# One gated MLP layer on one core: the second block's x transposed by DMA in 16-bit planes instead of by TensorE

## The chip, the cores and the metric

The kernel runs on one NeuronCore of a Trainium2 chip. The metric is the device time of one execution in microseconds (us); less is better. The engines are TensorE (PE in the profile; its weight loads are PEld), VectorE (DVE), ScalarE (ACT), GpSimd (POOL) and SyncE (SP), which issues all DMAs of this kernel from one queue, in order.

## The reference, cut to what matters

With D = 1024, E = 2048, 2048 positions and one layer, all in float32:

```python
mod = silu(c) @ ada_w + ada_b
shift, scale, gate = split(mod, 3)
h = rmsnorm(x, norm_g) * (1 + scale) + shift
u, v, z = split(h @ w_in, 3)              # 1024 -> 3 * 2048
u = gelu(u)
v = layernorm(gelu(v), ln_g, ln_b)        # over the 2048 columns
v = einsum("hpq,bnqhc->bnphc", sp_w, v)   # 128-position chunks, 8 head groups
v = v + sp_b
y = (u * v * silu(z)) @ w_out             # 2048 -> 1024
x = x + gate * y
return rmsnorm(x, final_g)
```

## The kernel before, in words

The 2048 positions are worked on in two blocks of TB = 1024 (b = 0 and 1). Each block first makes v (`project_v`), then a u and a z unit for each of 8 head groups (`project` for the products, `after` for the gating), sixteen units in all (NU = 16). The products use a Strassen scheme with seven products p1 to p7 of quarter matrices. Each float32 operand is split in a rounded part `hi` on ACT and a remainder `lo` on DVE (`split`, L168 and L169), and three matmuls of 128x512 stand for one (`mm3`, L178 to L180). Twelve such matmuls make one product of a unit. Four buffers each hold `hi` and `lo`. The output projection follows after both blocks.

`project_v` runs a list of steps. For block 0 the list `seq_0` is: p1 and p2 of v group 1 (`v1`), then p5, p6, p3, p7, p4 of group 0 (`v0`), then the same five of group 1. After step n it calls `hook_0(n)`, which issues loads, Strassen sums and, from n = 4 to 10, steps of the generator `preparations()`. The product p1 of group 1 of block 0 comes too early to be kept on the chip: it is stored in `c1_dram` ("spilled") and loaded again when p6 of this group is evicted (L496 to L500). In `evict`, p6 adds its PSUM bank to c1 and the sum to u4.

`finish` puts a piece of v through Gelu, takes its `bn_stats` (L516) and stores it in `v_dram`. `layer_norm` (L708) aggregates the statistics of the eight chunks of 128 positions with `bn_aggr` (L710) and makes mean and rstd, and `load_v` loads a head group of v again and normalizes it on ACT (L538).

`preparations()` prepares, beside block 0, what block 1 needs. After three steps for the spatial weights it runs `prepare_h(tp)` for the eight chunks tp of 128 positions of block 1. This loads x (128 x 1024) into the one buffer of the tag `hx`, normalizes it (`normalize_x`: Square with a running sum on ACT, L157; a power on POOL, L150; the product on DVE, L160), transposes it on PE in eight 128x128 pieces, four to a PSUM bank (L667), applies scale and shift on ACT out of PSUM (`modulate`, L253), and stores the result in `h_dram`. Later `prepare_sums` loads quarters of `h_dram`, forms Strassen sums and stores these, and at the last unit of block 0 `refill` loads them as the left operands of block 1. `preparations()` is advanced by `hook_0`, and then twice in each unit: in `after`, behind its second step, and at its end in `side`.

Short-lived tiles (products, gating results, the Square's output, transposed pieces, parts of sums) come from one ring of 15 buffers of 2 KB per partition (`c_tile`).

The order on each engine is laid down ahead of the run by the scheduler of the framework. It goes by the order in which the program names the operations and by its own idea of when each can start, so operations named later may stand ahead of ones that wait. At run time each engine and the DMA queue of SP keep to the order laid down.

Of the kernel before, what the change touches and what calls it, by code (L numbers as in the profile page):

```python
# [9 lines left out]
F32 = mybir.dt.float32  # L10
F32R = mybir.dt.float32r
BF16 = mybir.dt.bfloat16
AF = mybir.ActivationFunctionType
ALU = mybir.AluOpType
PSUM = bass.MemoryType.PSUM
# [2 lines left out]
P = 128  # L18
# [4 lines left out]
def kernel(  # L23
# [33 lines left out]
    nc = tc.nc  # L57

    T, D = x.shape
# [6 lines left out]
    KD = D // P  # L66
# [20 lines left out]
    def acc_bank(name):  # L87
        return acc.tile([P, 512], F32, tag="acc", name=name)

    def aux_bank(name):  # L90
        return aux.tile([P, 512], F32, tag="aux", name=name)
# [71 lines left out]
    def normalize_x(xt, name):  # L163
        for _ in normalize_steps(xt, name):
            pass
# [16 lines left out]
    def c_tile(name, shape=(P, HT), dt=F32):  # L182
        return cp.tile(list(shape), dt, tag="c", name=name)
# [68 lines left out]
    def modulate(out, src, k):  # L252
        nc.scalar.activation(  # L253
            out, src, AF.Identity, bias=mshift[:, k:k + 1], scale=mscale[:, k:k + 1]
        )
# [170 lines left out]
    class Group:  # L426
# [5 lines left out]
        def __init__(self, b, g):  # L432
            self.b, self.g = b, g
            self.name = f"{b}_v_{g}"
            self.q, self.c1, self.u4 = {}, {}, {}
            self.spilled = b == 0 and g == 1

        def load(self, r, f, slot):
# [26 lines left out]
        def multiply(self, p, k, w):  # L465
            if k == 0:
                self.po = [acc_bank(f"{p}_{ch}_{self.name}") for ch in range(HT // P)]
            hi, lo = S[Group.LEFT[p]][k]
            for ch, ps in enumerate(self.po):
                cs = slice(ch * P, (ch + 1) * P)  # L470
                mm3(ps, hi[:, cs], lo[:, cs], *w, k == 0, k == KH - 1)
            if k == KH - 1:
                for ch, ps in enumerate(self.po):
                    self.evict(p, ch, ps)

        def evict(self, p, ch, ps):
            def tile(name):
                return c_tile(f"{name}_{ch}_{self.name}", (P, FB))

            def add(t, s, o=None):  # L480
                nc.vector.tensor_tensor(t if o is None else o, t, s, op=ALU.add)  # L481

            if p == "p1":
                self.c1[ch] = tile("c1")
                nc.scalar.activation(self.c1[ch], ps, AF.Copy)
                if self.spilled:
                    nc.sync.dma_start(c1_dram[ch], self.c1[ch])
            elif p == "p2":
                t = tile("c11")
                add(self.c1[ch], ps, t)  # L490
                self.finish(0, 0, ch, t)
            elif p == "p5":
                self.u4[ch] = tile("u4")
                nc.scalar.activation(self.u4[ch], ps, AF.Copy)
            elif p == "p6":
                if self.spilled:  # L496
                    self.c1[ch] = tile("u2")
                    nc.sync.dma_start(self.c1[ch], c1_dram[ch])
                add(self.c1[ch], ps)
                add(self.u4[ch], self.c1[ch])  # L500
            elif p == "p3":
                t = tile("c12")
                add(self.u4[ch], ps, t)
                self.finish(0, 1, ch, t)
            elif p == "p7":
                add(self.u4[ch], ps)
                self.finish(1, 1, ch, self.u4[ch])
                add(self.c1[ch], ps)
            else:
                add(self.c1[ch], ps)  # L510
                self.finish(1, 0, ch, self.c1[ch])

        def finish(self, m, f, ch, t):
            i, n = 2 * self.g + f, m * (HT // P) + ch
            nc.scalar.activation(t, t, AF.Gelu_apprx_tanh)
            nc.vector.bn_stats(stats[:, n, i, :], t)  # L516
            nc.sync.dma_start(v_dram[i][:, n, :], t)

    def project_v(seq, hook, right=()):

# [133 lines left out]

    def prepare_h(tp):

        xt = vp.tile([P, D], F32, tag="hx", name=f"x_1_{tp}", bufs=1)
        t0 = TB + tp * P
        nc.sync.dma_start(xt, x[t0:t0 + P, :])
        normalize_x(xt, f"1_{tp}")  # L660
        yield
        for i in range(KD // 4):
            ps = aux_bank(f"psh_{tp}_{i}")
            ht = c_tile(f"ht_{tp}_{i}", (P, 4, P))
            for kk in range(4):
                k = 4 * i + kk
                nc.tensor.transpose(ps[:, kk * P:(kk + 1) * P], xt[:, k * P:(k + 1) * P], ident)  # L667
            for kk in range(4):
                modulate(ht[:, kk, :], ps[:, kk * P:(kk + 1) * P], 4 * i + kk)
            nc.sync.dma_start(h_dram[:, 4 * i:4 * i + 4, tp * P:(tp + 1) * P], ht)  # L670
            yield

    def prepare_sums(k):

        t = []
        for r, kk in ((0, k), (0, k + KH), (1, k), (1, k + KH)):
            t.append(c_tile(f"hq_{kk}_{r}"))
            nc.sync.dma_start(t[-1], h_dram[:, kk, r * HT:(r + 1) * HT])
        t.append(c_tile(f"hq_{k}_s"))
        strassen_sums(  # L680
            *t[:4], t[4], t[2], t[0], t[1],
            lambda i, s: nc.sync.dma_start(hs_dram[i][k], s),
        )
# [22 lines left out]


    def layer_norm():  # L708
        for ch in range(NCH):
            nc.vector.bn_aggr(mv[:, ch, :], stats[:, ch])  # L710
        nc.vector.tensor_scalar(lm, mv[:, :, 1], EPS, None, op0=ALU.add)
        nc.gpsimd.tensor_tensor(lr, lm, mhalf, op=ALU.pow)
        nc.vector.tensor_scalar(lm, mv[:, :, 0], -1.0, None, op0=ALU.mult)
        nc.gpsimd.tensor_tensor(lm, lm, lr, op=ALU.mult)
# [166 lines left out]
    def hook_0(n):  # L881

        if n == 0:
            v0.load(1, 1, "raw0")
        elif n == 1:
            v0.load(1, 0, "raw1")
        elif n == 3:
            v1.load(0, 0, "raw1")
        elif n == 4:
            v1.load(0, 1, "raw0")  # L890
        elif n == 5:
            v1.load(1, 1, "v1")
        elif n == 6:
            v1.load(1, 0, "v0")
        elif n == 10:
            units[0].load()
            units[0].p1()
        if n != 1:
            sums_0(n)
        for j in ahead_loads.get(n, ()):  # L900
            units[2 * j].ahead_load()
        if 4 <= n < 11:
            next(prep, None)
        if 8 <= n < 11:
            next(prep, None)

    def side(i):

        next(prep, None)
        if i in (4,6,9,11):  # L910
            prepare_sums((4,6,9,11).index(i))
        if 0 <= i - NU < KD:
            for db in range(NDB):
                prepare_gate(NDB * (i - NU) + db, gate_sum)
        elif i - NU == KD:
            finish_gate(gate_sum)
# [449 lines left out]
```

## Time and profile before

| what | value |
|---|---|
| median of 3 runs | 1339.7 us (1339.46 to 1340.07) |
| the profiled execution | 1338.98 us, its span 1337.2 us |
| PE busy | 1309.1 us, 98% of the span |
| DVE busy | 1078.7 us, 81% |
| ACT busy | 684.7 us, 51% |
| POOL busy | 25.6 us, 2% |
| DMA | 229.24 MB, mean 171 GB/s |

A time of the span starts at the first instruction of the profiled execution. A matmul's duration in the trace overlaps with the next one's, so what matmuls cost is read from the distance between their starts. The transposes of block 1's x run between 189 and 337 us of the span.

### The profile page before, as it was taken

How to read it: one execution, taken by the hardware profiler on the slowest of the kernel's cores; microseconds unless marked ns; L12 is line 12 of the kernel's file. 1: busy time of each engine (PE TensorE's matmuls, PEld its weight loads, DVE VectorE, ACT ScalarE, POOL GpSimd, SP SyncE). 2: the span in 40 equal slices, each digit the busy share in tenths (PEclk: the TensorE clock that was granted, in tenths of full speed). 3: DMA queues.
4: the chain of work that ended last, by engine and by line, in shares of the span. 5: the costliest groups of instructions: out<-in, count | busy, mean ns of one | idle time of the engine just before them, and what ended most of it. 6: DMA issues, size and time to landing. Idle time of an engine off the chain costs nothing.

```text
span 1337.2 us, 17243 instructions
## 1 busy us (share of the span) xinstructions
PE 1309.1 (98%) x6078; PEld 1088.8 (81%) x6078; DVE 1078.7 (81%) x1801; ACT 684.7 (51%) x1177; POOL 25.6 (2%) x42
## 2 busy tenths in 40 slices
PE   5999999999999999999999999999999999999998
PEld 4878877888888888888888888888888888888886
DVE  6889978888889888978688889887799944757875
ACT  5775446766545536534345555445543434344553
POOL 0000001000000000000000000000000000000101
PEclk9999999999999999999999999999999999999999
DMA  9771657456665446442243445434338722235733
GB/s 322 262 268 62 221 181 229 155 175 222 230 210 201 157 163 235 183 142 95 96 158 102 147 154 185 138 122 127 123 118 310 265 95 95 96 119 210 255 108 126
DMA packets 156799, 229.24 MB, mean 171 GB/s; under 512 B 9188, under 2 KB 91172, under 8 KB 153384
## 3 DMA queue, kind: packets, MB, share of 16 engines
q1 hardware_dynamic: 156712, 228.14, 49.9%
q8 instruction: 47, 0.77, 0.2%
q14 instruction: 40, 0.33, 0.1%
HBM read 160.47 MB, written 67.64 MB: 171 GB/s over the span
## 4 chain that ended last, share of the span: by engine, by line
PE 77%; DVE 3%; DMA 2%; issue 1%; ACT 1%; POOL 0%; POOLq 0%; SPq 0%; DVEq 0%; ACTq 0%
PE p_z L180 7%; PE p_z L178 7%; PE p_z L179 7%; PE po L180 7%; PE po L179 7%; PE po L178 7%; PE p_u L180 6%; PE p_u L178 6%; PE p_u L179 6%; PE pmix_u L553 4%; PE p_v L178 4%; PE p_v L179 3%; PE p_v L180 3%; DMA vn<-v_dram 1%; DMA held<-g_dram 1%
## 5 line engine op out<-in xcount | busy, mean ns | idle before, releaser
L178 PE MATMUL p_v<-hi_p_v,sh 128*128 128x512 f32 x416 | 162.5, 391 | 2.9 <-DVE u_v L481 2.3
L180 PE MATMUL po<-hi_o,gl 128*128 128x512 f32 x416 | 161.9, 389 | 0.4 <-DVE gl L169 0.4
L179 PE MATMUL p_v<-lo_p_v,sh 128*128 128x512 f32 x416 | 162.3, 390 | 0.0
L180 PE MATMUL p_v<-hi_p_v,sl 128*128 128x512 f32 x416 | 162.3, 391 | 0.0
L179 PE MATMUL po<-lo_o,gh 128*128 128x512 f32 x416 | 161.8, 389 | 0.0
L178 PE MATMUL po<-hi_o,gh 128*128 128x512 f32 x416 | 161.8, 389 | 0.0
L168 ACT ACTIVATE gh<-gr 128x1024 fp32r<-128x1024 f32 x52 | 55.0, 1059 | 126.2 <-PE po L179 116.4
L168 ACT ACTIVATE hi_p_v<-b_v 128x512 fp32r<-128x512 f32 x104 | 65.0, 630 | 106.2 <-PE p_v L180 89.7
L169 DVE TENSOR_TENSOR gl<-gr,gh 128x1024 fp32r<-128x1024 f32 x52 | 63.5, 1222 | 60.0 <-ACT gh L168 59.8
L169 DVE TENSOR_TENSOR lo_p_v<-b_v,hi_p_v 128x512 fp32r<-128x512 f32 x104 | 69.9, 687 | 34.4 <-ACT hi_p_v L168 34.1
L178 PEld LDWEIGHTS p_v<-hi_p_v,sh 128*128 128x128 f32 x416 | 78.1, 188 | 20.3 <-DVE u_v L481 2.8
L180 PEld LDWEIGHTS po<-hi_o,gl 128*128 128x128 f32 x416 | 78.1, 188 | 16.9 <-DVE gl L169 0.8
L179 PEld LDWEIGHTS po<-lo_o,gh 128*128 128x128 f32 x416 | 78.1, 188 | 16.4
L178 PEld LDWEIGHTS po<-hi_o,gh 128*128 128x128 f32 x416 | 78.1, 188 | 16.2
L179 PEld LDWEIGHTS p_v<-lo_p_v,sh 128*128 128x128 f32 x416 | 78.1, 188 | 16.1 <-DVE lo_p_v L169 0.2
L180 PEld LDWEIGHTS p_v<-hi_p_v,sl 128*128 128x128 f32 x416 | 78.1, 188 | 16.0
L538 ACT ACTIVATE vn<-vn,lm,lr 128x256 f32<-128x256 f32 x128 | 67.7, 590 | 27.1 <-DMA vn<-v_dram 18.6
L180 PE MATMUL p_u<-sh,lo_p_u 128*128 128x512 f32 x196 | 76.5, 390 | 0.0
L179 PE MATMUL p_u<-sl,hi_p_u 128*128 128x512 f32 x196 | 76.3, 389 | 0.0
L178 PE MATMUL p_u<-sh,hi_p_u 128*128 128x512 f32 x196 | 76.3, 389 | 0.0
L178 PE MATMUL p_z<-sh,hi_p_z 128*128 128x512 f32 x192 | 74.9, 390 | 0.0
L180 PE MATMUL p_z<-sh,lo_p_z 128*128 128x512 f32 x192 | 74.7, 389 | 0.0
(244 smaller groups left out, 3096.5 us busy)
## 6 DMA issues: line engine op xcount, KB each, us to landing
gr<-g_dram SPq DMA_DIRECT2D x26, 1024.0 KB, 4.8
b_v<-in_gm_w_in_dram SPq DMA_DIRECT2D x18, 1024.0 KB, 6.1
vn<-v_dram SPq DMA_DIRECT2D x16, 1024.0 KB, 6.0
raw_u<-in_gm_w_in_dram SPq DMA_DIRECT2D x16, 1024.0 KB, 5.1
raw_z<-in_gm_w_in_dram SPq DMA_DIRECT2D x16, 1024.0 KB, 5.2
v_dram<-c_v SPq DMA_DIRECT2D x44, 256.0 KB, 2.7
g_dram<-c_u SPq DMA_DIRECT2D x37, 256.0 KB, 2.3
aw<-in_ada_w_dram SPq DMA_DIRECT2D x16, 512.0 KB, 5.1
```

The source lines that it names most:

```text
L168: nc.scalar.activation(hi, src, AF.Copy)
L169: nc.vector.tensor_tensor(lo, src, hi.bitcast(F32), op=ALU.subtract)
L178: nc.tensor.matmul(ps, lhsT=sh, rhs=mh, start=first, stop=False)
L179: nc.tensor.matmul(ps, lhsT=sh, rhs=ml, start=False, stop=False)
L180: nc.tensor.matmul(ps, lhsT=sl, rhs=mh, start=False, stop=last)
L538: nc.scalar.activation(vt[:, ch, :], vt[:, ch, :], AF.Identity, bias=lm[:, ch:ch + 1], scale=lr[:, ch:ch + 1],)
L553: nc.tensor.matmul(pm[:, i * P:(i + 1) * P], lhsT=vt[:, m * (NCH // 2) + i, f * P:(f + 1) * P], rhs=spT[:, u.j, :], start=True, stop=True,)
```

## The change

The changed kernel does four things otherwise.

- `prepare_h` no longer uses PE. After the normalization ACT copies the low and the high 16-bit halves of x's float32 words into two planes of 128 x 1024 16-bit numbers. Each plane is transposed by a DMA from SBUF to SBUF, issued by SP. In the next step POOL copies the two transposed planes, interleaved, back into the buffer of x, so that this now holds the transposed float32 numbers. ACT applies scale and shift in place, eight times 128x128, and one DMA stores all of it.
- The load of x is a step of its own in the generator, ahead of the normalization, so `prepare_h` has three steps, of which `preparations()` still takes two in one place. `hook_0` advances the generator seven times instead of ten, and `prepare_sums` runs at units 6, 8, 10 and 12 instead of 4, 6, 9 and 11.
- The spilled p1 is loaded again in p6's second slice k = 1, not at p6's eviction.
- The `bn_aggr` of a chunk is issued with the chunk's last `bn_stats` instead of in `layer_norm`.

```diff
-            self.q, self.c1, self.u4 = {}, {}, {}
+            self.q, self.c1, self.u4, self.left = {}, {}, {}, {}
...
         def multiply(self, p, k, w):
             if k == 0:
                 self.po = [acc_bank(f"{p}_{ch}_{self.name}") for ch in range(HT // P)]
+            if self.spilled and p == "p6" and k == 1:
+                for ch in range(HT // P):
+                    self.c1[ch] = c_tile(f"u2_{ch}_{self.name}", (P, FB))
+                    nc.sync.dma_start(self.c1[ch], c1_dram[ch])
...
             elif p == "p6":
-                if self.spilled:
-                    self.c1[ch] = tile("u2")
-                    nc.sync.dma_start(self.c1[ch], c1_dram[ch])
                 add(self.c1[ch], ps)
...
             nc.sync.dma_start(v_dram[i][:, n, :], t)
+            self.left[n] = self.left.get(n, 2) - 1
+            if self.g and not self.left[n]:
+                nc.vector.bn_aggr(mv[:, n, :], stats[:, n])
...
         nc.sync.dma_start(xt, x[t0:t0 + P, :])
+        yield
         normalize_x(xt, f"1_{tp}")
+        turned = []
+        for i in range(2):
+            plane = c_tile(f"plane_{tp}_{i}", (P, D), U16)
+            nc.scalar.activation(plane, xt.bitcast(U16)[:, i::2], AF.Copy)
+            turned.append(c_tile(f"turned_{tp}_{i}", (P, KD, P), U16))
+            nc.sync.dma_start_transpose(turned[i], plane)
         yield
-        for i in range(KD // 4):
-            ps = aux_bank(f"psh_{tp}_{i}")
-            ht = c_tile(f"ht_{tp}_{i}", (P, 4, P))
-            for kk in range(4):
-                k = 4 * i + kk
-                nc.tensor.transpose(ps[:, kk * P:(kk + 1) * P], xt[:, k * P:(k + 1) * P], ident)
-            for kk in range(4):
-                modulate(ht[:, kk, :], ps[:, kk * P:(kk + 1) * P], 4 * i + kk)
-            nc.sync.dma_start(h_dram[:, 4 * i:4 * i + 4, tp * P:(tp + 1) * P], ht)
-            yield
+        ht = xt.rearrange("p (k t) -> p k t", t=P)
+        for i in range(2):
+            nc.gpsimd.tensor_copy(ht.bitcast(U16)[:, :, i::2], turned[i])
+        for k in range(KD):
+            modulate(ht[:, k, :], ht[:, k, :], k)
+        nc.sync.dma_start(h_dram[:, :, tp * P:(tp + 1) * P], ht)
+        yield
...
     def layer_norm():
-        for ch in range(NCH):
-            nc.vector.bn_aggr(mv[:, ch, :], stats[:, ch])
...
         if 4 <= n < 11:
             next(prep, None)
-        if 8 <= n < 11:
-            next(prep, None)
...
-        if i in (4,6,9,11):
-            prepare_sums((4,6,9,11).index(i))
+        if i in (6, 8, 10, 12):
+            prepare_sums((6, 8, 10, 12).index(i))
```

## Rows read from the trace of the kernel before

**Rows 1.** The page: busy time and share of the span, by engine.
```profile
PE 1309.1 (98%) x6078; PEld 1088.8 (81%) x6078; DVE 1078.7 (81%) x1801; ACT 684.7 (51%) x1177; POOL 25.6 (2%) x42
```

**Rows 2.** Waits of PE: total us, times, longest.
```profile
PE p_v L178 <- DVE u_v L481: 2.3, 1, 2.3
PE psh L667 <- DVE x L160: 1.1, 2, 0.6
PE p_u L180 <- DVE lo_b_u L169: 0.9, 1, 0.9
```

**Rows 3.** Timeline of PE: start, us, line, operation, count.
```profile
210.72 0.40 PE L180 MATMUL p_v<-hi_p_v,sl 128*128 128x512 f32 x1
210.95 1.04 PE L667 MATMUL psh<-ident,x 128*128 128x128 f32 x8
211.74 0.48 PE L178 MATMUL p_v<-hi_p_v,sh 128*128 128x512 f32 x1
212.06 0.39 PE L179 MATMUL p_v<-lo_p_v,sh 128*128 128x512 f32 x1
...
249.92 1.05 PE L553 MATMUL pmix_u<-spT,vn 128*128 128x128 f32 x8
250.81 0.60 PE L667 MATMUL psh<-ident,x 128*128 128x128 f32 x4
251.17 0.48 PE L178 MATMUL p_z<-sh,hi_t_z 128*128 128x512 f32 x1
...
254.02 1.05 PE L553 MATMUL pmix_u<-spT,vn 128*128 128x128 f32 x8
254.83 0.48 PE L178 MATMUL p_z<-sh,hi_t_z 128*128 128x512 f32 x1
...
267.19 0.39 PE L178 MATMUL p_u<-sh,hi_b_u 128*128 128x512 f32 x1
```

**Rows 4.** Timelines of SP and DVE around the spilled product's reload.
```profile
186.31 2.64 SPq L498 DMA_DIRECT2D u_v<-c_dram  x4
...
192.34 0.69 DVE L481 TENSOR_TENSOR u_v<-u_v,p_v 128x512 f32<-128x512 f32 x1 [3.44 <-DMA u_v<-c_dram]
```

**Rows 5.** The chain that ended last, from 218.65 to 231.58 us (first, one, last).
```profile
218.68 0.15 DVE r_m L149
...
229.94 0.37 DVE mv L710 x2
...
231.58 0.50 PE p_u L180
```

**Rows 6.** Stretches: PE, PEld, DVE, ACT, POOL busy (instructions), clock, DMA share, GB/s.
```profile
183.00:232.00 49.00, 45.62 (x208) 36.26 (x207) 37.33 (x72) 28.83 (x59) 3.81 (x5) 1.00 0.72 239
232.00:271.00 39.00, 38.43 (x192) 32.09 (x191) 32.35 (x53) 28.09 (x55) 2.16 (x3) 1.00 0.51 168
...
310.00:349.00 39.00, 39.00 (x196) 32.95 (x195) 34.11 (x55) 25.39 (x49) 0.55 (x1) 1.00 0.61 192
```

**Rows 7.** Groups by line and shape: busy us, mean ns.
```profile
L168 ACT ACTIVATE gh<-gr 128x1024 fp32r<-128x1024 f32 x52 | 55.0, 1059 | 126.2 <-PE po L179 116.4 <-issue 7.2 <-DVE t_u L559 2.5
L253 ACT ACTIVATE ht<-psh,mshift,mscale 128x128 f32<-128x128 f32 x64 | 24.4, 457 | 2.5 <-PE psh L667 2.4
L160 DVE TENSOR_SCALAR x<-x,r 128x1024 f32<-128x1024 f32 x16 | 12.0, 751 | 6.8 <-POOL r L150 6.6
masks.py:199 POOL TENSOR_SCALAR_AFFINE_SELECT ident<-ident 128x128 f32<-128x128 f32 x1 | 0.3, 294 | 0.1
masks.py:197 POOL MEMSET ident<- 128x128 f32 x1 | 0.2, 205 | 0.3 <-POOLq L1345 0.3
```

**Rows 8.** Timeline of DVE: the remainder used by PE behind 267.19 us.
```profile
258.49 0.68 DVE L169 TENSOR_TENSOR lo_b_u<-raw_u,hi_b_u 128x512 fp32r<-128x512 f32 x1
```

**Rows 9.** DMA queue (packets, MB, share of 16 engines) and issues (count, KB, us to landing).
```profile
q1 hardware_dynamic: 156712, 228.14, 49.9%
...
hs_dram<-hq SPq DMA_DIRECT2D x12, 256.0 KB, 2.1
```

More of the change, by code (lines that the diff above doesn't have):

```diff
@@ L12 @@
 BF16 = mybir.dt.bfloat16
+U16 = mybir.dt.uint16
 AF = mybir.ActivationFunctionType
```

## The prediction

> **What bounds the kernel now.** I read the page first: PE is busy 98% of the span [rows 1], so time is gained where PE's work or its waits go away, and lost where a new wait reaches PE. Then the list of PE's waits: behind the start-up it waits three times in the stretch that the change touches, 2.3 us for the reload of the spilled product, 1.1 us (two times) for a normalized x ahead of its transposes, and 0.9 us for a remainder at the first u unit [rows 2]. The timeline of PE gives what a transpose costs between matmuls [rows 3]. The chain that ended last runs on PE except, here, from 218.68 to 231.5 us, where it is on DVE [rows 5]. The stretches tell how much room the other engines have: from 183 to 232 us DVE is busy 37.3 of 49 us, and in the pairs of a u and a z unit of 39 us it is busy 32 to 34 and ACT 25 to 28 [rows 6].
>
> **The transposes go from PE.** Without them a matmul starts 0.23 us after the one before (210.72 to 210.95). A run of 8 transposes holds back the next matmul by 211.74 - 210.95 = 0.79 us, and the matmul after that starts 0.32 us later, not 0.23: together 0.88 us [rows 3]. In front of the units there are three such runs: 2.6 us. In the units there are ten runs of 4. With one, behind a mix of 8, the next product starts 251.17 - 249.92 = 1.25 us after the mix, without one 254.83 - 254.02 = 0.81 us: 0.44 us each, 4.4 us in all [rows 3]. PE's two waits for x have nothing to wait for any more: 1.1 us [rows 2]. Sum: 8.1 us. Bounds: 7.0 us, if other waits take the place of these, and 8.4 us, if the short gaps ahead of two runs go as well.
>
> **The reload is issued earlier.** The four loads go out at 186.31 us, and the first eviction on DVE waits 3.44 us for them and starts at 192.34 us; this is PE's wait of 2.3 us, because no bank is free [rows 4, 2]. A product of this group takes four slices of twelve matmuls, 2.7 us each by the 0.23 us above; behind k = 1 three slices are still to be run, so the loads leave some 8 us earlier than the eviction asks for them. They took 6 us (186.31 to 192.34). I take the whole 2.3 us. Lower bound 0, if SP stands behind another wait at that time. The four tiles lie in the ring 8 us longer; I cost that at nothing because only the four sums of p5 are kept beside them.
>
> **The aggregates and the stretch where DVE sets the end.** Two of the aggregates stand in DVE's chain at 229.94 us with 0.37 us, and a normalization of the fourth chunk too [rows 5]. The new program runs two normalizations ahead of the units, not four: 2 x 0.75 us of DVE less [rows 7]. Against it stand POOL's copies of the first chunk, which are new work beside DVE. I take 0.5 of the 0.9 us that PE waits at the end of this chain [rows 2]; bounds 0 and 0.9.
>
> **What is added, and on whom.** ACT: two plane copies of 1024 elements a chunk, no such row exists; by a 128x1024 copy they take 1.06 us each [rows 7], 2.1 us a chunk and 17 us in all. The eight modulates stay, from SBUF now, by the row of before 0.46 us [rows 7]. In a pair of units two chunks are prepared: ACT goes from 25 to 28 us to some 30 to 32 of 39 us [rows 6]. Work that hides it: ACT and DVE run ahead of PE. The remainder made at 258.49 us belongs to the product that PE begins at 267.19 us, 8.7 us later [rows 8, 3]. If that cover were gone, a chunk would cost PE the 2.1 us, 17 us in all. POOL: two copies of 1024 16-bit elements. The nearest rows are a fill of 128 elements, 205 ns, and a select of 128 elements, 294 ns [rows 7], 1.6 to 2.3 ns an element with all fixed time in them; as an upper bound a copy takes 2.3 us, and as a lower 0.9 us, because a fixed part must be in the 205 ns. I take 1.4 us; POOL is idle there [rows 6]. SP: two transposes more a chunk, one store of 512 KB in place of two of 256 KB, and x's load, which must wait until the store has read the buffer; behind these stand weight loads and stores of the gating in the same queue. The transposes themselves have no row. Lower bound 2.1 us, the fastest landing of 256 KB [rows 9]. By the queue's row a packet takes 0.499 x 16 x 1337.2 us / 156712 = 68 ns of an engine; a plane in rows of 256 bytes is 1024 packets, 64 an engine, 4.4 us, and in single elements 131072 packets, 560 us, which no row excludes [rows 9]. I take 4.4 us, because a plane moves in pieces of 128 elements if its blocks are 128x128. Between the two steps of a chunk lie five products (of twelve matmuls, 2.7 us each), or four where a saved product is skipped: 11 to 14 us. The chain to the planes' end takes 1.06 (Square) + 0.75 + 2 x 1.06 = 3.9 us and some 1 us for the statistics and the power; two transposes bring it to 10 to 14 us. That is about as long as the distance, so the merge comes at its time or a little late, inside the cover of 8.7 us. For all this new work together I take 2 us on PE, 0.25 us a chunk; bounds 0, because the units' only PE waits in the list are those for x [rows 2], and 17 us.
>
> [...]
>
> **Sum.** 8.1 + 2.3 + 0.5 - 2.0 = 8.9 us. The profiled execution took 1338.98 us, of which 1337.2 us are the span; it would come to 1330.1 us. The median of the runs lies 0.7 us above it, so I predict 1339.7 - 8.9 = 1330.8 us.
>
> **The rivals.**
>
> *DVE gives back what PE gains* (17%). [...] I split this case 8, 5 and 4 over faster, same and slower. [...]
>
> *The transposes land later than the order allows for, and ACT stands before the modulates* (12%, slower 10, same 2). In-order queues make it a wait: behind the modulates stand the `hi` parts and evictions, behind the store on SP the weight loads. If the merge comes d us later than its place in the order, each chunk costs PE d - 8.7 us. It becomes slower than before at 8 x (d - 8.7) > 10.9, d over 10 us, which means a plane of about 10 us, not 4.4. At d = 13 us the time is 1339.7 - 10.9 + 34 = 1363 us. For it: the price of a transpose is unknown. Against it: the queue has room, its engines are busy half to three quarters of the time here [rows 6].
>
> *The gain is given back later* (8%, faster 6, same 2). The stage in front of the units gets shorter on PE, and the chain moves to DVE there: only the units' 4.4 + 1.1 us and part of the rest remain, 1334 to 1337 us.
>
> *The ring is full* (5%, same 3, slower 2). A chunk takes five of fifteen tiles, not three, and holds four of them through the transposes, while u, z and the next u hold up to twelve. A bank that finds no tile is not evicted, and PE waits; at 1 to 2 us a chunk the time is 1338 to 1346 us.
>
> **How the numbers follow.** The forecast has 58%. A measurement of this kernel tells 0.2%, 2.7 us, from no change. Faster (under 1337.0 us): 58 + 8 + 6 = 72%. Same: 5 + 2 + 2 + 3 = 12%. Slower (over 1342.4 us): 4 + 10 + 2 = 16%. The likeliest case's own range is 1327.5 us (all gains, no new wait: 8.4 + 2.3 + 0.9 = 11.6 us, and 0.6 us for an order that happens to fall better) to 1335 us. The range is 1327 to 1341 us: it leaves out the slower cases and 4% below.
>
> **What would show it.** Right: no transposes of `psh` on PE; PE's wait for the reload and its waits for x gone; the first u unit some 5 us earlier, the end of the seventh unit some 9 us earlier, and from there the same distances as before; transposes landing in under 5 us; ACT's modulates with no wait over 8 us. Wrong: PE waiting for `hi` or `lo` or an eviction between 190 and 380 us; DVE operations longer beside POOL's copies; ACT waiting for POOL, and POOL for the transposes, by 10 us and more; SP standing at a transpose or at x's load with weight loads behind it.

## The result and the profile after

The changed kernel takes 1360.2 us, the kernel before, measured beside it, 1339.6 us: ratio 1.0148, interval 1.0135 to 1.016. It is 20.6 us slower where 8.9 us less were forecast. The page of the changed kernel, engines and granted clock in 40 slices (in tenths of full speed; answers to [rows 1]):

```profile
PE 1311.4 (97%) x6014; PEld 1085.4 (80%) x6014; DVE 1084.9 (80%) x1801; ACT 700.6 (52%) x1193; POOL 48.2 (4%) x58
...
PEclk9999999998899999999999999999999999999999
```

The span went from 1337.2 to 1358.9 us, by 21.7. PE's time without work (span less busy) went from 28.1 to 47.5 us, by 19.4, and its busy time rose by 2.3 us although 64 transposes are gone [rows 1]. Its four longest groups of waits from 150 to 540 us (answers to [rows 2]):

```profile
PE p_z L179 <- DVE c_u L321: 12.8, 2, 7.5
PE p_z L181 <- DVE lo_p_z L170: 3.2, 3, 1.4
PE p_z L179 <- ACT c_z L378: 2.2, 2, 1.1
PE p_u L181 <- DVE lo_t_u L170: 1.3, 1, 1.3
```

The waits of [rows 2] for the reload and for x are gone, as forecast. In their place stand two long waits for `c_u`, the sum with a saved product (the p1 of a u unit, made ahead, kept in DRAM and loaded again by SP, L375), and a number of short ones. Stretches (answers to [rows 6]):

```profile
232.00:271.00 39.00, 38.13 (x184) 31.50 (x183) 35.17 (x55) 28.95 (x54) 4.24 (x5) 1.00 0.62 179
310.00:349.00 39.00, 30.92 (x137) 24.77 (x136) 28.47 (x43) 21.98 (x38) 6.82 (x6) 0.91 0.58 152
349.00:388.00 39.00, 31.21 (x135) 25.46 (x133) 25.56 (x40) 24.80 (x44) 4.22 (x4) 0.87 0.68 202
```

From 310 to 349 us PE is busy 30.9 us, not 39.0 [rows 6], and DVE and ACT do less work too: nobody is overloaded, everybody waits. The single operations cost about what was forecast. DMA issues (count, KB, us to landing), and POOL's group by line:

```profile
h_dram<-x SPq DMA_DIRECT2D x8, 512.0 KB, 3.2
x<-in_x_dram SPq DMA_DIRECT2D x7, 512.0 KB, 3.9
...
turned<-plane SPq DMA_TRANSPOSE x16, 3.9
```

```profile
L677 POOL COPY x<-turned 128x1024 uint16<-128x1024 uint16 x16 | 22.5, 1414 | 54.1 <-DMA turned<-plane 27.0 <-issue 9.0 <-ACT hi_t_u L169 6.7
```

A plane lands 3.9 us after its issue (4.4 taken), a copy on POOL takes 1.41 us (1.4 taken), a plane copy on ACT 1.05 us (1.06 taken). What the prediction did not look at is how they stand one behind the other. Timeline of one chunk in the changed kernel (several engines, in order of time):

```profile
277.46 0.33 SPq L665 DMA_DIRECT2D x<-in_x_dram  x1
280.98 1.06 ACT L158 ACTIVATE sq<-x 128x1024 bf16<-128x1024 f32 x1 [0.42 <-DMA x<-in_x_dram]
282.99 0.75 DVE L161 TENSOR_SCALAR x<-x,r 128x1024 f32<-128x1024 f32 x1 [0.67 <-POOL r L151]
283.77 1.06 ACT L671 ACTIVATE plane<-x 128x1024 uint16<-128x1024 uint16 x1 [1.12 <-DVE x L161]
284.86 5.10 SPq L673 DMA_TRANSPOSE turned<-plane  x2
...
294.34 1.35 POOL L677 COPY x<-turned 128x1024 uint16<-128x1024 uint16 x1 [1.00 <-DMA turned<-plane]
295.72 1.27 ACT L254 ACTIVATE x<-x,mshift,mscale 128x128 f32<-128x128 f32 x3 [6.69 <-POOL x L677]
298.85 2.02 ACT L254 ACTIVATE x<-x,mshift,mscale 128x128 f32<-128x128 f32 x5
300.93 0.54 SPq L680 DMA_DIRECT2D h_dram<-x  x1
304.16 0.33 SPq L665 DMA_DIRECT2D x<-in_x_dram  x1
```

From one load of x to the next it is 26.7 us, and at each link something waits for the one before. Over all chunks, the list of waits from 183 to 420 us has SP for the store's reading of x (15.3 us, 7 times), ACT for x (8.2), ACT's planes for DVE (9.9), SP's transposes for the planes (19.8), POOL for the transposes (27.0), ACT's modulates for POOL (23.9), SP's store for the modulates (34.1 us, 8 times). It is a loop through the one buffer `hx`. A pair of a u and a z unit took 39 us [rows 6]; a unit, to which the program ties one chunk, is thus 19.5 us at most.

How that reaches PE, at its longest wait (timelines of ACT, SP, DVE and PE of the changed kernel):

```profile
365.45 1.04 ACT L671 ACTIVATE plane<-x 128x1024 uint16<-128x1024 uint16 x1
...
363.55 4.21 SPq L673 DMA_TRANSPOSE turned<-plane  x2
367.81 0.58 SPq L375 DMA_DIRECT2D c_u<-c_dram  x1
...
370.60 0.69 DVE L321 TENSOR_TENSOR c_u<-p_u,c_u 128x512 f32<-128x512 f32 x1 [1.28 <-DMA c_u<-c_dram]
...
371.43 0.76 PE L179 MATMUL p_z<-sh,hi_p_z 128*128 128x512 f32 x1 [7.45 <-DVE c_u L321]
372.00 0.63 PE L180 MATMUL p_z<-sl,hi_p_z 128*128 128x512 f32 x1
372.42 0.63 PE L181 MATMUL p_z<-sh,lo_p_z 128*128 128x512 f32 x1
```

The second transpose waits on SP for its plane, and behind it stands the reload of a saved product that belongs to a unit; DVE cannot add, the bank is not free, PE waits 7.45 us. At 322.79 us (5.34 us) the way is another one: by the chain that ended last it goes back over DVE and ACT to a load of weights that went out at 306.72 us, when `lo_t_u` was done, and took 8.1 us. That ACT's 6.69 us before the modulates made this load late is my reading; the chain does not show it. The chain that ended last runs on PE between such places, and enters PE each time from another side; it does not follow the loop all round.

### The profile page after: what moved, and what is told of

Read it like the earlier page. It is cut to its first block, busy times and chain, and to the rows that moved or that the text cites. A ratio compares the mean times of both kernels' runs of the same rounds, so it can differ in the third digit from the quotient of the medians.

```text
span 1358.9 us, 17198 instructions
## 1 busy us (share of the span) xinstructions
PE 1311.4 (97%) x6014; PEld 1085.4 (80%) x6014; DVE 1084.9 (80%) x1801; ACT 700.6 (52%) x1193; POOL 48.2 (4%) x58
## 3 DMA queue, kind: packets, MB, share of 16 engines
q1 hardware_dynamic: 173480, 232.34, 51.4%
## 4 chain that ended last, share of the span: by engine, by line
PE 82%; DVE 6%; DMA 4%; ACT 3%; issue 2%; POOL 1%; SPq 0%; POOLq 0%; DVEq 0%; ACTq 0%
PE p_z L179 7%; PE p_z L181 7%; PE p_z L180 7%; PE po L181 7%; PE po L180 7%; PE po L179 7%; PE p_u L179 6%; PE p_u L180 6%; PE p_u L181 6%; PE p_v L179 5%; PE p_v L181 5%; PE p_v L180 5%; PE pmix_u L558 4%; DMA x<-in_x_dram 1%; PE p L181 1%
## 5 line engine op out<-in xcount | busy, mean ns | idle before, releaser
L180 PEld LDWEIGHTS p_v<-lo_p_v,sh 128*128 128x128 f32 x416 | 78.1, 188 | 17.2 <-DVE lo_p_v L170 1.3
L179 PE MATMUL p_z<-sh,hi_p_z 128*128 128x512 f32 x192 | 77.6, 404 | 14.0 <-DVE c_u L321 12.8
L180 PE MATMUL p_z<-sl,hi_p_z 128*128 128x512 f32 x192 | 76.8, 400 | 0.0
```

Of the source, the lines that this page charges most:

```text
L179: nc.tensor.matmul(ps, lhsT=sh, rhs=mh, start=first, stop=False)
L180: nc.tensor.matmul(ps, lhsT=sh, rhs=ml, start=False, stop=False)
```

## The experiments

### The parts by themselves

The early reload alone, in the kernel before:

```diff
+            if self.spilled and p == "p6" and k == 1:
+                for ch in range(HT // P):
+                    self.c1[ch] = c_tile(f"u2_{ch}_{self.name}", (P, FB))
+                    nc.sync.dma_start(self.c1[ch], c1_dram[ch])
...
-                if self.spilled:
-                    self.c1[ch] = tile("u2")
-                    nc.sync.dma_start(self.c1[ch], c1_dram[ch])
```

> The kernel before with one part of the change alone: the spilled product is loaded again in p6's slice k = 1, not at its eviction. If the 2.3 us that PE waited for this reload are a gain of their own, the time is 1337.3 us (2.3 us under the kernel before, ratio 0.998). Rival: the wait comes back at the next place where DVE sets the end (the chain at 218 to 231 us of the trace of before), and the time stays within 0.5 us of 1339.6 us.

Measured: 1340.4 us against 1339.8 (ratio 1.0005, 0.9996 to 1.0013): nothing. Timeline of SP in this run:

```profile
180.57 0.35 SPq L660 DMA_DIRECT2D x<-in_x_dram  x1
185.35 0.53 SPq L537 DMA_DIRECT2D vn<-v_dram  x1
185.93 2.55 SPq L471 DMA_DIRECT2D u_v<-c_dram  x4
```

The loads leave at 185.93 us as before [rows 4], since a load of x and one of v stand ahead of them. In the changed kernel they leave at 170.57 us. The new place of the reload in the code isn't what does this, as two later runs show (below); nor is it the missing transposes, because with x turned by TensorE again (next run) they leave at 169.19 us too. What is left of the change in this stretch are the aggregates and the steps of x's preparation, with three `next(prep)` less in `hook_0` and x's load a step of its own.

The changed kernel with x turned by TensorE again:

```diff
-            nc.sync.dma_start_transpose(turned[i], plane)
...
-            nc.gpsimd.tensor_copy(ht.bitcast(U16)[:, :, i::2], turned[i])
+                nc.tensor.transpose(ps[:, kk * P:(kk + 1) * P], xt[:, k * P:(k + 1) * P], ident)
+                modulate(ht[:, 4 * i + kk, :], ps[:, kk * P:(kk + 1) * P], 4 * i + kk)
```

> The changed kernel with x turned by TensorE again (8 transposes through two banks of PSUM in the step of the merge, no planes, no DMA transposes, no copies on POOL); its order of steps, its one store of 512 KB, the early reload, the aggregates and the places of the sums stay. Theory (the round trip ACT, SP, DMA, POOL, ACT within one step makes the queues stand): without the trip nothing stands, the reload's 2.3 us and some of the waits for x (1.1) are kept, the 7.0 us of transposes come back: 1336 to 1339 us. Rival (the new order of steps does the harm: eight modulates in a row on ACT, one store in place of two and x's load behind it): 1350 us or more, with PE waits for c_u or lo_p_z of 5 us as in the changed kernel.

Measured: 1340.9 us against 1339.7 (1.0008, 0.9998 to 1.0017), above the 1336 to 1339 us of its theory. So the other edits do no harm, and without the DMA transposes they gain nothing either; the loss belongs to the trip through planes, DMA and POOL.

### Which resource

The transposes issued from ACT's queue, and, in a second kernel, the modulates on POOL:

```diff
-            nc.sync.dma_start_transpose(turned[i], plane)
+            nc.scalar.dma_start_transpose(turned[i], plane)
```

```diff
-            modulate(ht[:, k, :], ht[:, k, :], k)
+            nc.gpsimd.tensor_scalar(
+                ht[:, k, :], ht[:, k, :], mscale[:, k:k + 1], mshift[:, k:k + 1],
+                op0=ALU.mult, op1=ALU.add,
+            )
```

> The changed kernel, with the DMA transposes issued by ACT, behind its own plane copies, not by SP. Theory A, SP's queue: the transposes that wait for a plane hold up what stands behind them in SP's queue (a reload of a saved product, the weights), and PE's wait of 7.5 us at 371 us with the half clock after it comes from that; then the time falls by 8 to 14 us to 1346 to 1352 us, although ACT has 16 issues more. Theory B, ACT's queue: ACT stands before the modulates until POOL has merged the planes (23.9 us in the trace); then the time is within 4 us of 1360 us, or above it. Theory C, DVE stands while POOL copies: within 4 us of 1360 us as well.

> The changed kernel, with scale and shift applied by POOL behind its merge, not by ACT: ACT never waits for POOL. Theory B (ACT stands before the modulates, 23.9 us): PE's waits between 296 and 416 us shrink to a few us, and the time falls by 12 to 20 us to 1340 to 1348 us. Theory A (SP's queue): the wait at the transposes stays, 1354 to 1360 us. Theory C (DVE stands while POOL works): POOL works 64 operations more, and the time rises above 1362 us.

Measured: 1375.5 us (1.0269, 1.0247 to 1.0291) and 1362.9 us (1.0175, 1.0161 to 1.0189). With SP relieved the longest waits of PE are for ACT's eviction `c_z` (17.2 us), with 10.5 us still for `c_u`; with ACT relieved they are for DVE's `t_u` (13.4 us). Relieving either queue alone takes nothing off the time. Each of the two kernels puts the work on another queue, though, so they do not show what a queue costs by itself.

The two copies of a chunk on ACT, otherwise as changed:

```diff
-            nc.gpsimd.tensor_copy(ht.bitcast(U16)[:, :, i::2], turned[i])
+            nc.scalar.activation(ht.bitcast(U16)[:, :, i::2], turned[i], AF.Copy)
```

> The changed kernel with the two copies of a chunk on ACT, everything else as it is. In the changed kernel ACT waits 6.7 us (median) for POOL ahead of the modulates, and POOL 7.3 us for the transposes; a pair of copies takes 2.6 to 3.5 us on POOL there. Theory (distance): ACT waits some 3 us less and works 2.1 to 2.8 us more, so it stands as long as before: 1354 to 1362 us. [...]

Measured: 1367.2 us (1.0209, 1.0195 to 1.0223), above the forecast of 1354 to 1362 us, with PE waits of 5.2 to 5.8 us at 323, 345, 374 and 396 us. DVE's busy time falls from 1084.9 to 1078.7 us, that of before, so POOL's copies do lengthen DVE's work by some 6 us; but that is not what makes the kernel slow.

### More steps for a chunk

One empty step between the transposes and the merge, the sums at units 10 to 13:

```diff
             next(hs[tp - 1])
             yield
+            yield
             next(hs[tp - 1])
...
-        if i in (6, 8, 10, 12):
-            prepare_sums((6, 8, 10, 12).index(i))
+        if i in (10, 11, 12, 13):
+            prepare_sums((10, 11, 12, 13).index(i))
```

> The changed kernel with one empty step more between a chunk's transposes and its merge, so that a chunk takes three steps of the generator (about a unit and a half), and the sums of block 1 follow at units 10 to 13. The work is the same, and so are POOL's copies. If the queues' waits (theories A and B) come from too short a distance between a chunk's two steps, they vanish, and the gain that was predicted comes out: 1330 to 1336 us. Theory C (DVE stands while POOL copies): the copies are as long and as many, and the time stays over 1350 us.

Measured: 1336.0 us (0.9975, 0.9964 to 0.9986), 24 us off the changed kernel. PE's waits from 150 to 520 us:

```profile
PE p_z L179 <- ACT hi_p_z L169: 5.2, 2, 5.0
PE p_u L181 <- DVE lo_p_u L170: 0.6, 1, 0.6
```

The same boundary placed between the normalization and the planes, one `next(hs[tp - 1])` more to go with it:

```diff
         normalize_x(xt, f"1_{tp}")
+        yield
         turned = []
```

> The changed kernel with three steps a chunk and not two, as in the run with one step more, but the added boundary lies between the normalization and the planes, not behind the transposes; the sums again at units 10 to 13. The trip behind the step (planes 2.1, issue and landing some 6 to 8, copies 2.8 us) then starts without the 4 us of Square, power and scaling ahead of it. If the whole distance from x's landing to the merge is what counts: 1334 to 1337 us, as with the other boundary. If the distance from the planes to the merge counts: ACT still waits for POOL 2 to 5 us a chunk and the time lies between, 1338 to 1348 us.

Measured: 1338.8 us (0.9992, 0.9983 to 1.0002). Wherever the step is put, more than 20 us come back. It lies at the lower end of its second range (1338 to 1348 us), 2.8 us above the run before, and the intervals of the two just touch, so the distance from the planes to the merge may have a small share; that is not shown.

Both boundaries, and three steps a unit in place of two, so that a chunk comes every 4/3 units; and the same with the reload at the eviction again:

```diff
-            if n == 1:
+            if n in (0, 2):
                 next(prep, None)
```

> The changed kernel with four steps a chunk: normalization, planes and transposes, nothing, merge; a unit takes three steps and not two, so a chunk comes every 4/3 units, the sums at units 10 to 13. Theory (only the distance was wrong, the prices of the single operations right): ACT waits under 1 us for POOL, no PE wait over 2 us between 290 and 430 us, 1328 to 1333 us, the gain that was forecast. Rival (the added work on ACT, 17 us, or POOL's copies beside DVE cost by themselves): not under 1335 us.

> The run with two steps more, but the saved product's reload is issued at the eviction again, as in the kernel before. Tells the worth of the early reload once nothing else stands. If its 2.3 us are a term of their own: 2.0 to 2.6 us over the run with two steps more. If the wait goes anyway, because x's load and the transposes no longer stand ahead on PE: 0 to 0.5 us.

Measured: 1346.5 us (1.0045, 1.0031 to 1.0059) and 1346.8 us (1.0051, 1.0038 to 1.0063). The first misses its forecast of 1328 to 1333 us. Its timeline, POOL, DVE and PE:

```profile
201.07 1.38 POOL L678 COPY x<-turned 128x1024 uint16<-128x1024 uint16 x1 [12.06 <-PE p_v L181]
...
420.72 6.97 POOL L678 COPY x<-turned 128x1024 uint16<-128x1024 uint16 x2 [5.18 <-ACT vn L543]
422.31 0.68 DVE L573 TENSOR_TENSOR c_z<-c_u,c_z 128x512 f32<-128x512 f32 x1
422.91 0.69 DVE L204 TENSOR_TENSOR c_u<-u_z,u_z 128x512 f32<-128x512 f32 x1
424.84 1.66 DVE L204 TENSOR_TENSOR c_u<-c_z,u_u 128x512 f32<-128x512 f32 x1
...
431.48 0.79 PE L179 MATMUL p_u<-sh,hi_t_u 128*128 128x512 f32 x1 [4.39 <-ACT hi_t_u L169]
432.07 0.63 PE L180 MATMUL p_u<-sl,hi_t_u 128*128 128x512 f32 x1
432.49 0.63 PE L181 MATMUL p_u<-sh,lo_t_u 128*128 128x512 f32 x1
```

Two copies take 6.97 us where DVE runs additions with both operands in SBUF (0.69 us each, one of them 1.66), 5.35 us at 340.92 us, and 2.7 to 3.6 us elsewhere (the expectations below say 2.7). So the copies went to ACT, with one step more and with two:

> The run with one step more, but the two copies of a chunk that put the turned planes together (1024 16-bit elements each) are made by ACT, not POOL. In the trace of the run with two steps more, two copies on POOL took 6.97 us (420.72) and 5.35 us (340.92) where DVE ran additions with both operands in SBUF, and 2.7 us elsewhere; in the run with one step more the worst pair took 3.38 us (311.70). Theory (POOL's copies are only held up where DVE is dense, and with one step more the merges fall elsewhere): the time stays about as with one step more, 1335 to 1338 us, since ACT now works 2.1 to 2.8 us more a chunk where it waited 4.6 us. Rival (the copies on POOL are the part of the trip that is too long everywhere): 1332 us or less. Other rival (ACT is the bound): 1340 us or more.

> The run with two steps more, with the two copies of a chunk on ACT. Theory: its two stalls on PE (2.5 us at 350 us, 4.4 us at 431 us, with matmuls at half the clock behind them) come from POOL copies that stood beside DVE's additions (5.35 and 6.97 us for a pair, 2.7 us elsewhere); without POOL they go: 1330 to 1336 us. Rival (the third step in a unit makes the steps come too close together on ACT, whoever copies): 1343 us or more, the same stalls.

Measured: 1337.0 us (0.9982, 0.9974 to 0.9991) and 1333.4 us (0.9956, 0.9942 to 0.997). Both meet their forecasts, and the second is the fastest so far. Its page, and PE's longest waits from 150 to 540 us:

```profile
PE 1301.3 (98%) x6014; PEld 1081.1 (81%) x6014; DVE 1076.8 (81%) x1801; ACT 718.6 (54%) x1209; POOL 24.9 (2%) x42
```

```profile
PE p_z L181 <- DVE lo_p_z L170: 0.8, 1, 0.8
PE p_z L179 <- ACT hi_p_z L169: 0.7, 2, 0.4
PE p_v L179 <- DVE u_v L486: 0.6, 1, 0.6
```

No wait is left over 0.8 us there. The second block's first product starts at 527.30 us, at 537.17 before and at 558.42 in the changed kernel. The profiled execution took 1329.6 us.

In all these runs with more steps the sums come later too (units 10 to 13), and no run moved them alone in the changed kernel. Its trace speaks against their part in it. Timelines of PE and SP of the changed kernel, then of PE in the run with two steps more and the copies on ACT, each with the second mix of the fourth head group:

```profile
391.21 1.05 PE L558 MATMUL pmix_u<-spT,vn 128*128 128x128 f32 x8
398.25 1.55 SPq L688 DMA_DIRECT2D hq<-h_dram  x2
```

```profile
360.41 1.05 PE L558 MATMUL pmix_u<-spT,vn 128*128 128x128 f32 x8
```

The changed kernel is 30.8 us behind at this mix, of 31.1 us in the end, and its first sum loads `h_dram` only afterwards. Of the 30.8 us 5.4 are there at the first mix of all (244.20 against 238.83 us), ahead of which the changed kernel normalizes two chunks and this run one; these 5.4 us are not the pace in the units.

The same kernel with the reload at the eviction again:

> The run with two steps more and the copies on ACT (1333.4 us), with the saved product's reload issued at the eviction again, as in the kernel before. If the early issue is worth its 2.3 us: 1335 to 1337 us, and the loads leave SP some 10 us later. If it is only what stands ahead of the loads in SP's queue that counts (in the run with two steps more and the late reload the loads left at 169.06 us, with the early one at 170.47): 1332 to 1335 us, no difference.

Measured: 1333.5 us (0.9958, 0.9944 to 0.9971). The timeline of SP has the loads at 169.52 us although the code asks for them at the eviction:

```profile
169.52 1.80 SPq L499 DMA_DIRECT2D u_v<-c_dram  x4
177.67 0.62 SPq L540 DMA_DIRECT2D vn<-v_dram  x1
180.00 0.34 SPq L664 DMA_DIRECT2D x<-in_x_dram  x1
```

### Distance or pace

My theory up to here was the distance between a chunk's two steps. It was tried at an unchanged pace, two steps and a chunk a unit: the merge one product later (`n == 2`, shown), one earlier (`n == 0`), and all steps one call later, which swaps the two steps' places:

```diff
-            if n == 1:
+            if n == 2:
                 next(prep, None)
```

```diff
         next(hs[0])
         yield
+        yield
         for tp in range(1, NCH + 1):
```

> The changed kernel with the merge one product later in the unit (before p4, not before p7): six products of 2.7 us between normalization and merge, not five; still two steps a chunk and a chunk a unit. If the distance sets the loss (five products 1360 us, seven with one step more 1336 us): 1340 to 1352 us. If the place among the evictions sets it: no such order, within 5 us of 1360 us or slower.

> The changed kernel with the merge one product earlier (before p3): four products between normalization and merge. If the distance sets the loss: 1366 to 1382 us. If the place sets it: 1360 us or less.

> The changed kernel with all of x's steps one call later, so that the normalization falls before p7 and the merge before p2: two products between them, and five between x's load and its normalization, the other way round than in the changed kernel. If the distance sets the loss: slower than with four products, 1380 us or more. If the place sets it (ACT blocked before p7, where it must evict for the next product): faster than 1360 us, since the merge no longer falls there.

Measured: 1360.9 us (1.0159, 1.0142 to 1.0176), 1352.3 us (1.0094, 1.0077 to 1.0111) and 1365.0 us (1.0181, 1.0162 to 1.0201). Six products 1361, five 1360, four 1352, two 1365: the theory falls as the one cause. The rival in these expectations, the place of the merge among the evictions, is met by the first two runs and missed by the third. In the third 20 us are one wait. Its SP, DVE and PE:

```profile
406.06 0.55 SPq L680 DMA_DIRECT2D h_dram<-x  x1
...
409.33 0.80 SPq L688 DMA_DIRECT2D hq<-h_dram  x2
410.17 0.42 SPq L375 DMA_DIRECT2D c_u<-c_dram  x1
...
412.18 0.69 DVE L204 TENSOR_TENSOR hq_s<-hq,hq 128x512 f32<-128x512 f32 x1 [11.81 <-DMA hq<-h_dram]
...
415.86 0.77 PE L179 MATMUL p_z<-sh,hi_p_z 128*128 128x512 f32 x1 [20.04 <-DVE c_u L321]
```

The first sum reads what the last chunk has only just stored, and the reload of the saved product stands behind it in SP's queue. So next the place in SP's queue was tried: in the changed kernel the reload of the saved product goes ahead of the step that issues the transposes; with the steps swapped, the sums come one unit later (7, 9, 11, 13); then both:

```diff
         u.p4()
         change(A22)
+        if i < len(units) - 1 and units[i + 1].saved and (i + 1) % NU:
+            units[i + 1].p1()
         next(rest, None)
```

> The changed kernel with the reload of a u unit's saved product (p1, L375) issued one step earlier, ahead of the step that normalizes x and issues the transposes. If the place of this reload in SP's queue makes the loss: the wait of 7.45 us at 371 us goes, with 2.6 us of matmuls at half the clock behind it, perhaps the one of 5.34 us at 323 us too: 1342 to 1351 us. If ACT's late merge makes it by itself: the waits go to hi_p_z or c_z and the time stays at 1356 to 1362 us.

> The run with the steps swapped, with the four sums one unit later (7, 9, 11, 13), so that the first sum's read of h_dram no longer follows the last merge in the same step. The wait of 20.04 us at 416 us should go with the 2.6 us behind it: 1341 to 1346 us from 1365. If something else holds the reload there: 1355 us or more.

> The run with the steps swapped, the sums one unit later and the saved product's reload ahead of the transposes: still two steps a chunk, a chunk a unit and two products between them. If it is the queue behind late transfers that costs (SP's reload, SP's and DVE's sums): the wait of 5.58 us at 354 us goes as well, 1331 to 1338 us. If the short distance costs by itself: 1345 us or more.

Measured: 1361.7 us (1.0163, 1.0143 to 1.0183), 1354.3 us (1.0106, 1.0091 to 1.0121) and 1356.2 us (1.0119, 1.01 to 1.0137). The timeline of PE in the first:

```profile
366.86 0.47 PE L179 MATMUL p_z<-sh,hi_p_z 128*128 128x512 f32 x1 [0.59 <-DVE u_u L321]
...
388.59 0.79 PE L179 MATMUL p_z<-sh,hi_b_z 128*128 128x512 f32 x1 [10.32 <-ACT c_z L378]
```

The wait of 7.45 us for `c_u` at 371 us is gone, and 10.32 us for ACT's eviction have come at 388 us; the time stays. That is what the second theory of this run had, ACT's late merge; but the kernel with the modulates off ACT was no faster either. Without the sums behind the merge 10.8 us come back of the 20, short of the forecast 1341 to 1346 us, and with the reload ahead as well nothing more comes. Whichever item is freed, the next one waits. The three runs with the merge before p3 or p2 that aren't held up by a sum (1352.3, 1354.3 and 1356.2 us) lie 4 to 8 us under the changed kernel, so the place among the evictions may account for that much; no run isolates it.

The runs side by side, without the early reload alone and the two runs with the late reload; the interval is the mean of the last five from one chunk's Square on ACT to the next one's:

```
                                   units a chunk  interval us  time us
changed kernel                           1          25.5       1360.2
 transposes issued by ACT                1          28.5       1375.5
 modulates on POOL                       1          25.2       1362.9
 copies on ACT                           1          27.0       1367.2
 merge one product later, earlier        1       25.4, 23.9    1360.9, 1352.3
 swapped; sums later; both               1    23.4, 23.5, 23.9 1365.0, 1354.3, 1356.2
 saved reload ahead                      1          25.4       1361.7
 turned by TensorE                       1          20.1       1340.9
two steps more                          1.33        27.0       1346.5
 and copies on ACT                      1.33        25.1       1333.4
one step more; other boundary           1.5     30.2, 29.6     1336.0, 1338.8
 and copies on ACT                      1.5         29.7       1337.0
```

In the run with two steps more and the copies on ACT the first mixes of the u units stand at 275.1, 313.3, 349.5 and 387.6 us: 18.75 us a unit, 25.0 us for 1.33 units. A chunk every 25.1 us is just what that pace asks for. At a chunk a unit it may take 18.75 us; no order with the trip in it came under 23.4.

## Why the prediction was wrong

**The step that failed** is the overlap at the end of the part on what is added: "That is about as long as the distance, so the merge comes at its time or a little late, inside the cover of 8.7 us." Between 183 and 420 us ACT stood 23.9 us before the modulates for the merge, SP 34.1 us before the stores for the modulates, and PE lost 12.8 us in two waits for a sum behind late transfers. The term that hangs on this step, 2 us for all the new work, came to 26.8 us (1360.2 us against 1333.4 us in the run with more steps, a slower pace and the copies on ACT).

Why it failed is in part argued. I held half of a chunk's way (Square to the turned planes, 10 to 14 us) against half of a unit, and covered what was over with a lead that can be spent once. What had to be held against a unit is the whole way round the one buffer `hx`, as each load of x waits for the store that reads it. My own numbers give it: 4.9 us to the planes' end, 4.4 or 8.8 us for two transposes (overlapped or not), a copy of 1.4, eight modulates of 0.46 are 14.4 to 18.8 us, and with the store and the load as they were measured (3.2 and 3.9) 21.5 to 25.9 us, against at most 19.5 us of a unit [rows 6]. That the load waits for the store stands in the prediction; it wasn't added up. The chunk shown above gives an estimate of the way without any standing: 3.5 us from the load to the Square, 2.8 to the first plane, 2.1 for the planes, 3.9 for the second transpose, 1.35 for its copy, 3.3 for the modulates and 3.2 for the store, some 20 us. So the bare way is longer than a unit of 18.75 to 19.5 us by little, and of the measured 25.5 us some 5 are standing in the queues.

**How far this is shown.** Shown by runs: the trip makes the loss (with TensorE 1340.9 us); relieving SP, ACT or POOL singly, or another distance in products, does not take it away; more steps and a slower pace do (1336.0, 1338.8, 1333.4 us, and 1346.5 us where POOL's copies stood). Only argued: that the way round `hx` is what the pace runs into. For it speaks that every link waits for the one before, and that with the modulates off ACT the interval stayed at 25.2 us, so that ACT's load is not the limit. Against it, the chain that ended last does not follow the loop all round. The intervals of the table alone prove little, because a chunk is tied to a unit, and the interval grows whatever PE waits for. The direct test, a second buffer for x, wasn't run. This theory came last and foretold no run, so the cause behind the failed step stays open. Why four products between the steps cost 8 us less than five stays open too.

**The gains.** Transposes off PE: right. PE's busy time falls from 1309.1 us to 1301.3 in the run with two steps more and the copies on ACT, 7.8 us for 64 transposes (7.0 taken; the 1.1 us of PE's waits for x are no busy time). In the changed kernel it is 10.1 us more than that for the same 6014 instructions. The granted clock is 0.91 and 0.87 in the two stretches with the long waits and 1.00 from 232 to 271 us; behind the wait of 7.45 us eleven matmuls start 0.43 us apart, where 0.23 us is usual, and the granted clock is 0.50 from 372 to 376 us (1.00 again from 376.6 to 382 us). So this long wait was paid twice, which the prediction didn't count.

Reload: the wait went, but by another edit. Alone the early issue is worth nothing (1340.4 us), and taken back out it costs nothing (1346.8 against 1346.5, 1333.5 against 1333.4 us). Aggregates and DVE's chain: nothing is seen of the 0.5 us, at its end PE waits 1.30 us for `lo_t_u` (229.43 us) where it waited 0.9 for `lo_b_u` [rows 2]. The first mix of the units came 2.1 us earlier than before (244.20 against 246.30 us), not some 5. The run with two steps more and the copies on ACT reached the sum as a whole in its profiled execution (1329.6 us, 1330.1 forecast), but that is the fastest of its five; its median of 1333.4 us is 5.9 us under the kernel before, not 8.9, and two of the terms are not seen where they were put. That it comes so near is in part luck.

**The rivals.** The second, late transposes and queues that stand, names the right waits, and its example of 1363 us is near; its condition, a plane of about 10 us, was not met: the transposes land in 3.9 us. By the account above it erred because it too let the lead of 8.7 us cover every chunk afresh. The first rival, DVE giving back what PE gains beside POOL's copies, had 17% by the author's estimate; no row of before has such copies. The runs show it in part, and mostly the other way round: in the run with two steps more it was POOL that stood, 6.97 us for its pair at 420.72 us beside DVE's additions, of which one took 1.66 us and not 0.69, and 13 us went when the copies moved to ACT (1346.5 to 1333.4 us). In the changed kernel itself a pair of copies took 2.6 to 3.5 us, so it decides nothing there.

## What to carry to other kernels

Where work is threaded through a loop step by step, add up the whole way round its buffer, from load to the load that replaces it, and compare it with the time of one turn of the loop; a lead covers the difference once, not each turn. That this sum decided here is argued, not shown. When freeing one late item moves the wait to another and the time stays, stop looking for the queue at fault and look at the pace. With the transposes on the DMA queue TensorE's busy time was 7.8 us shorter here (1301.3 us in the run with two steps more and the copies on ACT), but give their round trip several steps: one step more was worth 24 us (1360.2 against 1336.0 us).

## What the runs showed of the hardware

In the changed kernel a DMA transpose of a 128x1024 plane of 16-bit elements from SBUF to SBUF lands in 3.9 us (2.8 to 4.5) and holds SP 1.26 us for the issue, as against 0.33 us for x's load. The queue moved 16768 packets more than before (173480 against 156712) for sixteen planes, all under 512 B: 1048 a plane, near the 1024 rows of 256 bytes from which the 4.4 us were taken. A copy of 1024 16-bit elements with stride 2 at the output takes 1.41 us on POOL (changed kernel) and 1.37 us on ACT (two steps more, copies on ACT); beside a dense run of DVE additions from SBUF in the run with two steps more the pair on POOL took 5.35 us (340.92 us) and 6.97 us (420.72 us), while DVE's additions beside the second pair took 0.68 and 0.69 us and one 1.66. In the same run, behind a wait of 4.39 us, matmuls start 0.42 us apart (432.07 to 432.49 us); in the changed kernel, behind the wait of 7.45 us, it is 0.43 us at a granted clock of 0.50.
